# Hyena mixer of a hybrid encoder: Pool's elementwise work moves to VectorE, and a DMA that adds makes the weights' low parts

## The chip, the cores and the metric

The kernel runs on one core of one Trainium2 chip. The metric is the device time of one execution in microseconds; the time before is the median of three runs, and a change of 0.2% (2.5 us) is about what can be told from no change.

The engines are named as in the profile: PE (TensorE, matrix products; PEld is its weight load), DVE (VectorE), ACT (ScalarE), POOL (GpSimd) and SP (SyncE, which here only issues DMAs). They run their own instruction lists in order and wait for each other through semaphores. 16 DMA engines move data between HBM and the on-chip memory.

## The reference

The input is 256 tokens of 1024 channels in float32. Four layers follow, each `x = x + mixer(rmsnorm(x))`, then `x = x + swiglu(rmsnorm(x))`. The mixers are A, B, C, A: A is a gated short convolution, B is neighbourhood attention, C is Hyena. What matters here is A's and C's short convolution, and C's long one:

```python
def short_conv_mixer(h, w_in, conv_w, w_out):
    b_gate, c_gate, u = jnp.split(h @ w_in, 3, axis=-1)
    return (b_gate * depthwise_conv3(c_gate * u, conv_w)) @ w_out
...
def hyena_mixer(h, w_in, short_w, short_b, ...):
    v, x1, x2 = jnp.split(depthwise_conv3(h @ w_in, short_w, short_b), 3, axis=-1)
    h_freq = hyena_filters(seq, ...)
    def long_conv(u, n):
        y = irfft(rfft(u, n=2 * seq) * h_freq[:, n], n=2 * seq)[:, :seq]
        return y + u * f_skip[n]
    z = x1 * long_conv(v, 0)
    z = x2 * long_conv(z, 1)
    return z @ w_out
```

## The kernel before, in words

**Weights in two parts.** Every weight is streamed once from HBM in pieces of [128, 1024] float32 (512 KB). `wload` (L95) makes of a piece `st` two operands of float32r, a format of fewer bits that PE takes at full rate: ACT writes `hi`, the piece rounded (L105), and DVE, or POOL for a share of the pieces, writes `lo = st - hi` (L109, through the helper `tt`, L74). A product is then three matmuls (`mm3`, L113): hi by x's high part (L116), hi by x's low part (L117), lo by x's high part (L118). A piece makes 24 matmuls. There are 5 buffers for `st` and 6 each for `hi` and `lo`; a buffer is written again when its last reader is done.

**The spectra of the filters** are computed beside the first two SwiGLUs and kept in HBM (`hf`).

**Mixer C** runs at about 626 to 781 us. Its work is a list of pieces: 24 of `c_w_in`, numbered 0 to 23 here, then 8 of `c_w_out`, 24 to 31. After each piece `line.tick()` runs the stages that are due (`Pipeline`, L236; slots in `HYENA_SLOTS`, L44). The first four pieces are multiplied side by side, as the residual's tiles come in; then follow the norm's statistics (`stats`, L158, in which POOL computes 1 / rms as `rtm`, L171) and `expand` (L173). Channels go by quarters q of 256. `short(i, q)` scales the product (`cp`, DVE) and convolves each half with `conv3` (L331). `spectrum(o, q)` multiplies by the transform's matrix (`uf`, PE), then by the filter's spectrum `H` (tiles `hq`): with `U`, `a`, `b` of [128, 1024], DVE does two sums U (L74), the products a and b, and U's first half from a; POOL does U's second half from b and the two halves of the folded result `a`. `back` transforms back (`yi`, PE, L734 and L738), and `gate` multiplies by the next signal. `conv3` is one ACT instruction for the middle tap, one DVE `scalar_tensor_tensor` for the first (L338), one ACT instruction into `cr` for the third (L341), and one POOL addition of `cr`. In mixer C from tick 9 on, POOL makes 0.6 of the low parts.

**Mixer A** uses `conv3` too, once for each of 8 channel tiles in each of two layers, and has nothing else on POOL but the norm.

A scheduler sets the order on every engine from the order of the code and its own estimates, so the order can differ from that of the source.

Of the kernel before, what the change touches and what calls it, by code (L numbers as in the profile page):

```python
# [13 lines left out]
ALU = mybir.AluOpType  # L14
# [15 lines left out]
# columns of the per-partition vector table  # L30
# [9 lines left out]
# Where the stages of the pipelined work lie, in slots of one weight piece each.  # L40
FILTER_SLOTS = (range(0, 19, 2), range(2, 17, 2))  # within the first and the second SwiGLU
ATT_LAGS = (3, 0, 4, 5, 8, 11)  # bias, normed, features, scores, turned, values_out
V_LAG = 3
HYENA_SLOTS = (4, 5, 8, 11, 13, 16, 19)  # into, (spectrum, back, gate) twice  # L44
NORM_LAG = 1
AHEAD = 6  # rows of an output projection that are taken as they come
# The share of the weights' low parts that the Pool engine makes, where DVE has much to do
POOL_FILTERS, POOL_HYENA, POOL_HYENA_FROM = 0.17, 0.6, 9
# [3 lines left out]
def encoder(ctx: ExitStack, tc: tile.TileContext, A: dict, out: bass.AP):  # L52
# [23 lines left out]
    def v2(a):  # L76
        """[P, 512] as two halves."""
        return a.rearrange("p (i t) -> p i t", i=2)

# [13 lines left out]
    share, count = [0], [0]  # L93

    def wload(src, n, tag="", cuts=((0, None, None),)):  # L95
        """A piece of a weight, [P, n], as two float32r parts. It may be loaded in
        cuts (from, to, what else to do after it)."""
        st = wst.tile([P, D], F32, tag="st", name=f"st{tag}")
        hi = wsp.tile([P, D], F32R, tag="hi", name=f"hi{tag}")
        lo = wsp.tile([P, D], F32R, tag="lo", name=f"lo{tag}")  # L100
        for c0, c1, then in cuts:
            c = slice(c0, c1 or n)
            for dst, s in src if isinstance(src, list) else [(slice(None), src)]:
                sy.dma_start(out=st[dst, c], in_=s[:, c])
            ac.copy(out=hi[:, c], in_=st[:, c])  # L105
            count[0] += 1
            pool = int(count[0] * share[0]) > int((count[0] - 1) * share[0])
            tt(lo[:, c], st[:, c], hi[:, c].bitcast(F32), ALU.subtract, gp if pool else ve)
            if then is not None:  # L109
                then()  # L110
        return hi, lo
# [8 lines left out]
    def split(hl, src):  # L120
        """hl[:, 0] + hl[:, 1] = src, both float32r; the parts lie along axis 1."""
        ac.copy(out=hl[:, 0], in_=src)
        tt(hl[:, 1], src, hl[:, 0].bitcast(F32), ALU.subtract)

    class Norm:
        """The pre-norm of the next sub-layer: x times the gain as the operand of
        its products, and 1 / rms by token for what comes out of them."""
# [30 lines left out]
        def stats(self):  # L158
            """1 / rms, the tokens on the partitions."""
            n = self.name  # L160
            for m in self.late:
                self.square(m)
            ps = self.ps = bank(f"psn{n}")
            ms = tp.tile([P, 2], F32, tag="ms", name=f"ms{n}", bufs=2)
            for i in range(2):
                pe.transpose(ps[:, i * P : (i + 1) * P], self.ss[:, i * P : (i + 1) * P], ident)
            ve.tensor_reduce(out=ms, in_=ps[:, :T].rearrange("p (i f) -> p i f", i=2), axis=AX.X, op=ALU.add)
            ve.tensor_scalar(out=ms, in0=ms, scalar1=1.0 / D, scalar2=EPS,
                             op0=ALU.mult, op1=ALU.add)
            rt = self.rt = tp.tile([P, 2], F32, tag="rt", name=f"rt{n}", bufs=2)  # L170
            gp.tensor_tensor(out=rt, in0=ms, in1=nhalf[:, :2], op=ALU.pow)  # L171

        def expand(self):  # L173
            """1 / rms along the tokens, on every partition."""
            n, ps, rt = self.name, self.ps, self.rt
            for i in range(2):
                pe.transpose(ps[:, T + i * P : T + (i + 1) * P], rt[:, i : i + 1].broadcast_to([P, P]), ident)
            self.R = tp.tile([P, T], F32, tag="R", name=f"R{n}", bufs=2)
            ac.copy(out=self.R, in_=ps[:, T:])
# [9 lines left out]
    def in_tile(ps, w, norm):  # L189
        """One 128-column tile of a product with the normed input."""  # L190
        for n, (k, xs) in enumerate(norm.xs.items()):
            mm3(ps, w, slice(k * P, (k + 1) * P), xs[:, 0], xs[:, 1], n == 0, n == KT - 1)

    def in_group(parts, norm):
        """Several column tiles side by side, for the first products after a norm:
        (accumulator, weight, whether it is the first of its bank)."""
# [5 lines left out]
    class OutProj:  # L202
        """x += mid @ w, the rows of w as they come."""
# [20 lines left out]
        def finish(self, mids, norm):  # L224
            for k in range(self.ahead, KT):
                self.load(k)
            for m in [*range(0, KT, 2), *range(1, KT, 2)]:  # neighbours share a bank
                for k in range(self.ahead, KT):
                    self.mul(m, k, mids[k])
                residual(m, self.acc[m // 2][:, (m % 2) * T : (m % 2 + 1) * T], norm)  # L230
# [5 lines left out]
    class Pipeline:  # L236
        """Work in stages, each some slots after the one before it."""
# [12 lines left out]
        def tick(self):  # L250
            """The stages that are due, the oldest work first."""
# [60 lines left out]
    def triple(w, m, norm, name, ready, each=lambda i: None):  # L312
        """Column tiles m, KT + m, 2 KT + m. The first three with a norm go side by side,
        unless it is ready."""
# [16 lines left out]
    def conv3(y, src, wcol, step, m, bcol=None):  # L331
        """Depthwise convolution of width 3 along the tokens."""
# [7 lines left out]
        r = t1("cr")  # L340
        ac.activation(r, src, AF.Copy, scale=w[2])  # L341
        tt(y[:, : T - 1], y[:, : T - 1], r[:, 1:], ALU.add, gp)

# [32 lines left out]
    def mixer_b(norm, nxt):  # L376
        with tc.tile_pool(name="attc", bufs=1) as cp, tc.tile_pool(name="attw", bufs=2) as wp:
# [21 lines left out]
            def values(i, ps):  # L399
                """v of two head pairs, and for each block of query columns its keys (row by  # L400
                column) on the partitions."""
# [15 lines left out]
            def normed(m):  # L417
                """q and k by token, normed: the root mean squares of the tokens and of the
                heads in one factor."""
# [15 lines left out]
            def features(m):  # L435
                """q, the heads as blocks of a diagonal, and k, by feature."""
# [56 lines left out]
            def rows(k, ps, w, first):  # L493
                """Rows k of the weight: 256 columns of the product, by token."""
# [45 lines left out]
    hf = {(o, q): dram.tile([P, 2, 512], F32, name=f"hf{o}{q}") for o in range(2) for q in range(4)}  # L540

    def filters(cp, wp):
        """The filters' spectra at the 256 odd multiples of pi / 512: the lower 128
        from the sum, the upper 128 (mirrored, conjugate) from the difference of what
        the even and the odd times give."""
# [40 lines left out]
        # rows 0..63 the high part, rows 64..127 the low part  # L586
# [7 lines left out]
        for o in range(2):  # L594
            for q in range(4):
                if q % 2 == 0:
                    # two quarters of both directions
# [46 lines left out]
                # the skip is one more tap at time 0  # L644
# [8 lines left out]
    def mixer_c(norm, nxt):  # L653
        with tc.tile_pool(name="hyc", bufs=1) as cp, tc.tile_pool(name="hyw", bufs=2) as wp:
# [9 lines left out]
            def short(i, q, ps):  # L664
                """The short convolution of signal i of the quarter."""
# [7 lines left out]
            def by_time(q, i):  # L673
                """The signal with the times on the partitions, the even ones and the odd ones."""
# [24 lines left out]
            def spectrum(o, q):  # L699
                """The spectrum, times the filter's, folded for the even and the odd times."""  # L700
# [19 lines left out]
                tt(U[:, :, 1], b[:, :, 0], b[:, :, 1], ALU.add, gp)  # L720
                tt(a[:, 0], U[:, 0], U[:, 1], ALU.add, gp)
                tt(a[:, 1], U[:, 0], U[:, 1], ALU.subtract, gp)
                d["eo"] = a

            def back(o, q):
# [4 lines left out]
                for k in range(2):  # L730
                    for i in range(2):
# [3 lines left out]
                        else:  # L735
                            # by channel
# [14 lines left out]
            for i in range(3):  # L751
                for q in range(4):
                    ps = bank(f"ci{q}_{i}")
                    for j in range(2):
                        m = 2 * q + j
                        share[0] = POOL_HYENA if line.now >= POOL_HYENA_FROM else 0
# [18 lines left out]
            while line.todo:  # L775
                line.tick()
            op.finish(mids, nxt)

# [41 lines left out]
def _consts():  # L820
# [14 lines left out]
    # the frequencies below pi / 2; the others are their mirror images  # L835
# [4 lines left out]
    # [even times, odd times] x [frequency, (cosine, sine) by time]  # L840
# [20 lines left out]
    # what the sums of squares of q and of k are scaled by (the scores' 1 / 8 with q), and their guards  # L861
# [10 lines left out]
def _cols(w):  # L872
    """[L, K, N] -> [L, N / 128, 128 (K in), K / 128 * 128]: a column tile at a time."""
# [5 lines left out]
def _diagonals(rpb):  # L879
    """[heads, dr, dc] -> [head pair, (head parity, q row reversed, q column reversed),  # L880
    (block of q columns, k row, k column)]: shifted copies, so that each query has its row of biases."""
    w = np.lib.stride_tricks.sliding_window_view(rpb, 48, axis=2)[:, :, :16]
    w = np.stack([w[:, r + 4 : r + 4 + ROWS] for r in range(ROWS)])  # r, head, k row, i, j
# [4 lines left out]
def _layout(i):  # L888
# [5 lines left out]
    # by two head pairs: q and k of the one, of the other, then v of both  # L894
# [36 lines left out]
```

## Time and profile before

| | |
|---|---|
| runs | 1257.56, 1257.49, 1256.13 us; median 1257.49 |
| profiled execution | span 1256.2 us; its own time is not given apart from the span |
| PE | 1219.3 us busy, 97% of the span |
| DVE, ACT, POOL | 913.4 us (73%), 634.6 us (51%), 269.8 us (21%) |
| HBM read | 220.99 MB, 181 GB/s over the span |
| mean granted TensorE clock | 0.990 of full speed |

Busy time is an average over stages with different limits. The granted clock is the share of full speed that PE was given. Matmuls are pipelined: one of 256 columns shows about 280 ns from start to end, though the next starts about 120 ns after it. A row of waits names the instruction that waited, then the one that it waited for.

### The profile page before, as it was taken

The numbers are of one execution on the slowest core, as the hardware profiler recorded it, in microseconds if no ns is written. First come the engines' busy times: TensorE is split into PE (matmuls) and PEld (weight loads), VectorE is DVE, ScalarE is ACT, GpSimd is POOL, SyncE is SP. The second block draws the span as 40 slices with busy tenths as digits, with TensorE's granted clock in tenths as the row PEclk, the third lists the DMA queues.
The fourth block names the chain that finished last, engine by engine and source line by source line (L and its number), as shares of the span: only waits on it lengthen the run. The fifth ranks groups of instructions, "written<-read, shape, count | busy, mean of one in ns | idle before, by whom it ended". The sixth has DMA issues, their size and how long they took to land.

```text
span 1256.2 us, 24460 instructions
## 1 busy us (share of the span) xinstructions
PE 1219.3 (97%) x10034; PEld 1211.2 (96%) x10034; DVE 913.4 (73%) x1156; ACT 634.6 (51%) x931; POOL 269.8 (21%) x228
## 2 busy tenths in 40 slices
PE   7999999999999999999988979999999999999998
PEld 7999999999998999999988879999999999999998
DVE  7766877887776688878869997766655676766642
ACT  6545554555667554545544345444444455444431
POOL 0111122333454023213347773000000000000000
PEclk9999999999999999999998989999999999999999
DMA  9556556666666365666754324655566565655571
GB/s 307 184 175 229 185 173 193 201 191 222 209 178 194 118 218 186 192 187 191 232 179 135 121 98 155 199 184 185 173 185 197 176 188 163 199 185 185 170 203 46
DMA packets 68505, 228.90 MB, mean 182 GB/s; under 512 B 9831, under 2 KB 11241, under 8 KB 68265
## 3 DMA queue, kind: packets, MB, share of 16 engines
q1 hardware_dynamic: 61408, 211.68, 53.8%
q0 software_dynamic: 4656, 9.73, 2.6%
q10 hardware_dynamic: 2328, 5.93, 1.4%
q8 instruction: 78, 1.28, 0.4%
q14 instruction: 35, 0.28, 0.1%
HBM read 220.99 MB, written 6.29 MB: 181 GB/s over the span
## 4 chain that ended last, share of the span: by engine, by line
PE 84%; DVE 8%; issue 2%; ACT 2%; DMA 2%; POOL 2%; SPq 0%; ACTq 0%; DVEq 0%; POOLq 0%
PE pu L116 7%; PE pg L116 7%; PE pg L118 7%; PE pu L117 7%; PE pg L117 7%; PE pu L118 7%; PE po L116 7%; PE po L118 7%; PE po L117 7%; DVE a L74 1%; PE ai1a L117 1%; PE ai1a L116 1%; PE ai1a L118 1%; PE accao L116 1%; PE accao L117 1%
## 5 line engine op out<-in xcount | busy, mean ns | idle before, releaser
L105 ACT CAST hiw<-stw 128x1024 fp32r<-128x1024 f32 (+1 forms) x276 | 280.5, 1024 | 314.3 <-PE pg L117 85.3
L74 DVE TENSOR_TENSOR low<-stw,hiw 128x1024 fp32r<-128x1024 f32 (+1 forms) x254 | 306.2, 1212 | 155.1 <-ACT hiw L105 153.8
L116 PE MATMUL pu<-xsf,hiw 128*128 128x256 f32 x704 | 199.9, 284 | 0.0
L116 PE MATMUL pg<-xsf,hiw 128*128 128x256 f32 x704 | 199.3, 283 | 0.0
L118 PE MATMUL pg<-xsf,low 128*128 128x256 f32 x704 | 199.2, 283 | 0.0
L117 PE MATMUL pu<-xsf,hiw 128*128 128x256 f32 x704 | 199.2, 283 | 0.0
L117 PE MATMUL pg<-xsf,hiw 128*128 128x256 f32 x704 | 199.2, 283 | 0.0
L118 PE MATMUL pu<-xsf,low 128*128 128x256 f32 x704 | 199.2, 283 | 0.0
L116 PE MATMUL po<-hid,hiw 128*128 128x256 f32 x704 | 197.5, 281 | 0.0
L117 PE MATMUL po<-hid,hiw 128*128 128x256 f32 x704 | 197.5, 281 | 0.0
L118 PE MATMUL po<-hid,low 128*128 128x256 f32 x704 | 197.5, 281 | 0.0
L116 PEld LDWEIGHTS pg<-xsf,hiw 128*128 128x128 f32 x704 | 134.6, 191 | 0.3 <-issue 0.3
L116 PEld LDWEIGHTS pu<-xsf,hiw 128*128 128x128 f32 x704 | 134.5, 191 | 0.3 <-ACT hiw L105 0.3
L118 PEld LDWEIGHTS pg<-xsf,low 128*128 128x128 f32 x704 | 134.6, 191 | 0.0
L117 PEld LDWEIGHTS pg<-xsf,hiw 128*128 128x128 f32 x704 | 134.6, 191 | 0.0
L117 PEld LDWEIGHTS pu<-xsf,hiw 128*128 128x128 f32 x704 | 134.6, 191 | 0.0
L118 PEld LDWEIGHTS pu<-xsf,low 128*128 128x128 f32 x704 | 134.5, 191 | 0.0
L116 PEld LDWEIGHTS po<-hid,hiw 128*128 128x128 f32 x704 | 132.4, 188 | 0.0
L117 PEld LDWEIGHTS po<-hid,hiw 128*128 128x128 f32 x704 | 132.4, 188 | 0.0
L118 PEld LDWEIGHTS po<-hid,low 128*128 128x128 f32 x704 | 132.4, 188 | 0.0
L74 POOL TENSOR_TENSOR low<-stw,hiw 128x1024 fp32r<-128x1024 f32 (+1 forms) x22 | 53.6, 2434 | 158.8 <-ACT hiw L105 150.8
L105 ACT CAST hiai<-stai 128x1024 fp32r<-128x1024 f32 (+1 forms) x49 | 49.0, 1014 | 49.0 <-issue 13.3
(246 smaller groups left out, 2922.3 us busy)
## 6 DMA issues: line engine op xcount, KB each, us to landing
stw<-in_f_w SPq DMA_DIRECT2D x208, 512.0 KB, 3.6
stw<-in_f_w SPq DMA_DIRECT2D x64, 448.0 KB, 3.4
stai<-in_a_w_in SPq DMA_DIRECT2D x45, 512.0 KB, 3.7
stbi<-in_b_w_qkv SPq DMA_DIRECT2D x24, 512.0 KB, 4.3
stci<-in_c_w_in SPq DMA_DIRECT2D x24, 512.0 KB, 4.0
stao<-in_a_w_out SPq DMA_DIRECT2D x16, 512.0 KB, 4.3
hf<-ht POOLq DMA_DIRECT2D x16, 256.0 KB, 2.7
stbo<-in_b_w_out SPq DMA_DIRECT2D x8, 512.0 KB, 4.0
```

What stands on the lines that cost most here:

```text
L74: (eng or ve).tensor_tensor(out=out_, in0=a, in1=b, op=op)
L105: ac.copy(out=hi[:, c], in_=st[:, c])
L116: pe.matmul(ps, hi[:, ws], xh, start=first, stop=False, **kw)
L117: pe.matmul(ps, hi[:, ws], xl, start=False, stop=False, **kw)
L118: pe.matmul(ps, lo[:, ws], xh, start=False, stop=last, **kw)
```

## The change

Three things change (comments and docstrings, which the change also drops, are left out of the diff).

1. In `conv3`, in mixers A and C, the third tap becomes a second DVE `scalar_tensor_tensor`; ACT's `cr` and POOL's addition go.
2. In `spectrum`, POOL's three additions go to DVE.
3. In mixer C, for the pieces from tick 5 on (5 to 23 of `c_w_in` and 24 to 29 of `c_w_out`, 25 in all), neither DVE nor POOL makes the low part: ACT writes minus the rounded piece into `lo`, and a DMA issued by POOL reads the piece from HBM a second time and adds it to `lo` in place. The last two pieces are DVE's again.

```diff
-POOL_FILTERS, POOL_HYENA, POOL_HYENA_FROM = 0.17, 0.6, 9
+POOL_FILTERS = 0.17
+LOW_DMA_FROM = 5
...
             ac.copy(out=hi[:, c], in_=st[:, c])
+            if low_dma[0]:
+                ac.activation(lo[:, c], st[:, c], AF.Copy, scale=-1.0)
+                gp.dma_start(out=lo[:, c], in_=src[:, c], accum_op=ALU.add)
+                continue
             count[0] += 1
             pool = int(count[0] * share[0]) > int((count[0] - 1) * share[0])
             tt(lo[:, c], st[:, c], hi[:, c].bitcast(F32), ALU.subtract, gp if pool else ve)
...
         ve.scalar_tensor_tensor(out=y[:, 1:], in0=src[:, : T - 1], scalar=w[0], in1=y[:, 1:],
                                 op0=ALU.mult, op1=ALU.add)
-        r = t1("cr")
-        ac.activation(r, src, AF.Copy, scale=w[2])
-        tt(y[:, : T - 1], y[:, : T - 1], r[:, 1:], ALU.add, gp)
+        ve.scalar_tensor_tensor(out=y[:, : T - 1], in0=src[:, 1:], scalar=w[2], in1=y[:, : T - 1],
+                                op0=ALU.mult, op1=ALU.add)
...
-                tt(U[:, :, 1], b[:, :, 0], b[:, :, 1], ALU.add, gp)
-                tt(a[:, 0], U[:, 0], U[:, 1], ALU.add, gp)
-                tt(a[:, 1], U[:, 0], U[:, 1], ALU.subtract, gp)
+                tt(U[:, :, 1], b[:, :, 0], b[:, :, 1], ALU.add)
+                tt(a[:, 0], U[:, 0], U[:, 1], ALU.add)
+                tt(a[:, 1], U[:, 0], U[:, 1], ALU.subtract)
...
-                        share[0] = POOL_HYENA if line.now >= POOL_HYENA_FROM else 0
+                        low_dma[0] = line.now >= LOW_DMA_FROM
                         w = wload(A["c_w_in"][0][i * KT + m], D, f"ci{i}_{m}")
...
             while line.todo:
                 line.tick()
+            low_dma[0] = False
             op.finish(mids, nxt)
```

How the instructions move, at three places of mixer C. Lines of the changed kernel are 5 or 6 higher (its `tt` is L75, its `conv3` L343 to L346); in the names, the number after `loci_` is the channel tile.

POOL at the start of mixer C, before:

```order
L649 DMA hf_92<-ht_7770 128x512
L649 DMA hf_92<-ht_7773 128x512
L171 TENSOR_TENSOR rtm_8106<-msm_8101,nhalf 128x2
L74 TENSOR_TENSOR loci_1_8408<-stci_1_8406,hici_1_8407 128x1024
L74 TENSOR_TENSOR cx_0_8145<-cx_0_8145,cr 128x255 x2
```

and now, where L109 and L110 are the new ACT instruction and the new DMA:

```order
L654 DMA hf_92<-ht_7754 128x512
L654 DMA hf_92<-ht_7757 128x512
L110 DMA loci_5_8155<-in_c_w_in 128x1024
L110 DMA loci_6_8225<-in_c_w_in 128x1024
L177 TENSOR_TENSOR rtm_8090<-msm_8085,nhalf 128x2
L110 DMA loci_7_8264<-in_c_w_in 128x1024
```

Two of the adding DMAs stand ahead of the norm's `rtm`, and from there on POOL's list holds nothing but adding DMAs until the next norm.

ACT in the middle of mixer C, before:

```order
L105 CAST hici_6_8728<-stci_6_8727 128x1024
L741 COPY y_8392<-yi_8391 128x512
L122 CAST u_8398<-ut_0_8399 128x512
L704 DMA hq_8577<-hf_88 128x1024
L105 CAST hici_7_8765<-stci_7_8764 128x1024
L337 ACTIVATE cx_1_8438<-cp_1_8436,vec 128x256
L341 ACTIVATE cr<-cp_1_8436,vec 128x256
L337 ACTIVATE cx_1_8438<-cp_1_8436,vec 128x256
L341 ACTIVATE cr<-cp_1_8436,vec 128x256
L714 COPY e_8468<-uf_8451 128x512
```

and now:

```order
L106 CAST hici_6_8693<-stci_6_8692 128x1024
L746 COPY y_8364<-yi_8363 128x512
L128 CAST u_8370<-ut_0_8371 128x512
L109 ACTIVATE loci_6_8694<-stci_6_8692 128x1024
L106 CAST hici_7_8731<-stci_7_8730 128x1024
L709 DMA hq_8544<-hf_88 128x1024
L109 ACTIVATE loci_7_8732<-stci_7_8730 128x1024
L343 ACTIVATE cx_1_8411<-cp_1_8409,vec 128x256 x2
L719 COPY e_8437<-uf_8420 128x512
```

Each `hici` is followed, at once or after some instructions of the signals' chain, by the `loci` of the same piece, and the two `cr` are gone.

DVE for one spectrum and one short convolution, before:

```order
L74 TENSOR_TENSOR U_8593<-e_8596,uf_8586 128x512 x2
L74 TENSOR_TENSOR a_8594<-U_8593,hq_8577 128x1024
L74 TENSOR_TENSOR b_8595<-U_8593,hq_8577 128x1024
L74 TENSOR_TENSOR loci_2_8973<-stci_2_8971,hici_2_8972 128x1024
L74 TENSOR_TENSOR U_8593<-a_8594 128x2x256
L74 TENSOR_TENSOR cp_1_8674<-ci_1_8606,Rm_8141 128x512
L338 SCALAR_TENSOR_TENSOR cx_1_8676<-cp_1_8674,vec,cx_1_8676 128x255 x2
```

and now:

```order
L75 TENSOR_TENSOR U_8560<-e_8563,uf_8553 128x512 x2
L75 TENSOR_TENSOR a_8561<-U_8560,hq_8544 128x1024
L75 TENSOR_TENSOR b_8562<-U_8560,hq_8544 128x1024
L75 TENSOR_TENSOR cp_1_8643<-ci_1_8573,Rm_8125 128x512
L75 TENSOR_TENSOR U_8560<-a_8561 128x2x256
L75 TENSOR_TENSOR U_8560<-b_8562 128x2x256
L75 TENSOR_TENSOR a_8561<-U_8560 128x512 x2
L344 SCALAR_TENSOR_TENSOR cx_1_8645<-cp_1_8643,vec,cx_1_8645 128x255 x2
L346 SCALAR_TENSOR_TENSOR cx_1_8645<-cp_1_8643,vec,cx_1_8645 128x255 x2
```

The low part is gone from between the products and U's halves; U's second half, the two halves of `a` and the second `scalar_tensor_tensor` of each half have come.

## Rows read from the trace of the kernel before

**Rows 1.** The page: the span, and PE's busy time, share and instructions.
```profile
span 1256.2 us, 24460 instructions
...
PE 1219.3 (97%) x10034; PEld 1211.2 (96%) x10034; DVE 913.4 (73%) x1156; ACT 634.6 (51%) x931; POOL 269.8 (21%) x228
```

**Rows 2.** Windows: busy us (instructions) per engine, granted clock, DMA share and rate.
```profile
core 0: us, PE busy (x) PEld busy (x) DVE busy (x) ACT busy (x) POOL busy (x), PEclk, DMA share, GB/s
...
638.10:780.80 142.70, 123.95 (x902) 120.17 (x901) 127.89 (x125) 70.37 (x116) 97.37 (x63) 0.92 0.42 133
...
643.50:764.00 120.50, 103.14 (x728) 99.56 (x727) 110.82 (x102) 56.99 (x96) 91.98 (x61) 0.90 0.39 124
...
905.00:1005.00 100.00, 100.00 (x842) 100.00 (x841) 60.99 (x83) 47.26 (x64) 2.61 (x4) 1.00 0.61 185
...
610.00:620.00 10.00, 10.00 (x87) 10.00 (x87) 6.92 (x9) 4.40 (x6) 2.37 (x4) 1.00 0.90 306
```

**Rows 3.** Waits of PE, 638.1 to 780.8 us: total, times, longest.
```profile
PE yi L738 <- POOL a L74: 9.2, 5, 3.4
...
PE uf L117 <- DVE u L74: 5.5, 2, 3.0
...
PE psnm L177 <- POOL rtm L171: 1.4, 1, 1.4
```

**Rows 4.** Lines of DVE, 638.1 to 780.8 us: busy us, mean ns, idle before.
```profile
L338 DVE SCALAR_TENSOR_TENSOR cx<-cp,vec,cx 128x255 f32<-128x255 f32 x24 | 29.4, 1255 | 2.6 <-ACT cx L337 2.6
...
L74 DVE TENSOR_TENSOR a<-U,hq 128x1024 f32<-128x1024 f32 x8 | 19.8, 2477 | 0.2
...
L74 DVE TENSOR_TENSOR b<-U,hq 128x1024 f32<-128x1024 f32 x8 | 12.3, 1542 | 0.0
...
L74 DVE TENSOR_TENSOR loci<-stci,hici 128x1024 fp32r<-128x1024 f32 x9 | 11.9, 1324 | 9.0 <-ACT hici L105 9.0
...
L74 DVE TENSOR_TENSOR U<-a 128x512 f32<-128x512 f32 x8 | 8.4, 1051 | 0.2
```

**Rows 5.** DVE by tile, whole run: min/median/max ns, first and last start.
```profile
L74 DVE TENSOR_TENSOR a<-U,hq x8: 1225/2760/3452, 654.1 to 744.5; 128x1024 f32<-128x1024 f32 x8
...
L74 DVE TENSOR_TENSOR U<-a x8: 691/692/1784, 660.7 to 748.3; 128x512 f32<-128x512 f32 x8
...
L338 DVE SCALAR_TENSOR_TENSOR y<-u,vec,y x16: 476/478/480, 33.3 to 1042.5; 128x255 f32<-128x255 f32 x16
```

**Rows 6.** ACT and POOL by tile, whole run: min/median/max ns, first and last start.
```profile
L341 ACT ACTIVATE cr<-cp,vec x24: 492/493/497, 644.8 to 760.4; 128x256 f32<-128x256 f32 x24
...
L105 ACT CAST hici<-stci x24: 1032/1047/1057, 614.0 to 723.6; 128x1024 fp32r<-128x1024 f32 x24
...
L74 POOL TENSOR_TENSOR y<-y,cr x16: 637/640/645, 33.9 to 1043.1; 128x255 f32<-128x255 f32 x16
```

**Rows 7.** DMA: 638.1 to 764 us (two rows), 612 to 620 us, POOL's issue.
```profile
DMA packets 4258, 15.62 MB, mean 124 GB/s; under 512 B 464, under 2 KB 464, under 8 KB 4248
...
stw<-in_f_w SPq DMA_DIRECT2D x3, 512.0 KB, 3.3
...
dfth<-in_dfth POOLq DMA_DIRECT2D x1, 512.0 KB, 6.7
...
L656 POOL DMA_DIRECT2D dfth<-in_dfth x1: 564/564/564, 611.7 to 611.7; - x1
```

**Rows 8.** Timeline of POOL and of DVE about 621 us: start, duration, instruction.
```profile
621.00 1.15 POOL L649 DMA_DIRECT2D hf<-ht  x2 [1.02 <-DVE ht L74]
...
621.23 1.22 DVE L74 TENSOR_TENSOR loci<-stci,hici 128x1024 fp32r<-128x1024 f32 x1
```

**Rows 9.** Timeline of ACT and POOL at 637 us; PE by tile, mixer C's last products.
```profile
637.08 3.90 ACT L105 CAST hici<-stci 128x1024 fp32r<-128x1024 f32 x4 [8.67 <-PE ci L117]
...
641.01 1.61 POOL L171 TENSOR_TENSOR rtm<-msm,nhalf 128x2 f32<-128x2 f32 x1 [18.86 <-DVE msm L168]
...
L118 PE MATMUL accco<-midC,loco x64: 279/281/285, 758.2 to 780.6; 128*128 128x256 f32 x64
```

More of the change, by code (lines that the diff above doesn't have):

```diff
@@ L90, in encoder @@
     sy.dma_start(out=vec, in_=A["vec"])
-    share, count = [0], [0]
+    share, count, low_dma = [0], [0], [False]
     def wload(src, n, tag="", cuts=((0, None, None),)):
```

## The prediction

> **What bounds the kernel now.** I read the page first: PE is busy 1219.3 us of a span of 1256.2 us [rows 1], so only a stage in which PE waits or runs at a lower clock can give anything. The windows show the stage. From 905 to 1005 us PE is never idle and its granted clock is 1.00. From 638.1 to 780.8 us, mixer C from the norm on, it is busy 123.95 us of 142.7 at a mean granted clock of 0.92, a mixture of its two levels, 2.4 and 1.2 GHz [rows 2]. That is 18.75 us of idle time, and some 0.08 x 142.7 = 11.4 us that full clock would give back. PE's own work there is thus about 123.95 - 11.4 = 112.5 us.
>
> Next, who ends PE's waits: mostly POOL's halves of `a` (9.2 us) and DVE's `u` (5.5 us) [rows 3]. DVE is nearly full: 110.82 us of the 120.5 from 643.5 to 764 us [rows 2]. It is full because its instructions are long. The convolution's `scalar_tensor_tensor` takes 1255 ns, product a 2477 ns, b 1542 ns and U's half 1051 ns [rows 4], where the same instruction takes 478 ns in mixer A, and a and U's half 1225 and 691 ns at their shortest [rows 5]. POOL is busy 97.37 us of this stage and 2.61 us of the 100 from 905 us [rows 2]. So DVE is stretched while POOL works, and PE waits for the two of them.
>
> **The change, part by part.** All sums stand against the profiled span, 1256.2 us; the median of the runs is 1257.49, 1.3 us more. I subtract gains from the median.
>
> *Mixer A.* DVE gains 16 x 478 ns = 7.6 us over two layers, ACT loses 16 `cr` of the same form as the row shown, at 493 ns, and POOL loses 16 x 640 ns [rows 5, 6]. I cost it at nothing: the second mixer A lies around 1000 us, where PE is never idle while DVE is busy only 61 us in 100 [rows 2], and the chain from u to z loses one engine. Without that cover it would cost 7.6 us at most.
>
> *DVE in mixer C.* Without POOL's arithmetic the stretch goes: 24 x (1255 - 478) = 18.6 us, a 8 x (2477 - 1225) = 10.0, b 8 x (1542 - 1225) = 2.5 (a's form), U 8 x (1051 - 691) = 2.9, the low parts 9 x (1324 - 1220) = 0.9 [rows 4, 5, 8], together 34.9. These nine low parts themselves go: 9 x 1.22 = 11.0. Added are 24 `scalar_tensor_tensor` at 478 ns = 11.5 us and 24 half sums (8 for U, 16 for a) at 691 ns = 16.6 us. DVE goes from 127.9 to about 127.9 - 34.9 - 11.0 + 28.1 = 110 us.
>
> *ACT.* 25 more passes over a piece at 1.05 us, less 24 `cr` at 0.49 us [rows 6]: +14.5 us, from 70.4 to about 85 of 142.7 us. It stays off the path. What stands behind ACT's new instruction are the signals' casts, but it needs `st`, which is there already, and a `lo` buffer that PE frees with the same piece's `hi`, for which ACT waits before as well.
>
> *POOL.* 97 us of arithmetic become 25 issues at 0.56 us [rows 7]. `rtm` now stands behind two adds. The second needs piece 6's new pass. ACT reaches piece 6 at 637.1 us, as the row of four casts shows [rows 9], and is done with both passes at 639.2; the add is issued by 639.8. In the run before `rtm` began at 641.01 [rows 9], so nothing is lost.
>
> *The adds.* They load the DMA queues, and here lies the uncertainty. In mixer C from 638.1 to 764 us 15.62 MB move, 1.57 of them the next SwiGLU's three pieces [rows 7], which can come later: 14.05 MB are needed. 24 adds of 0.524 MB follow 639.8 us: 12.6 MB, times f, what an added byte costs against a loaded one. No row shows an adding DMA. The lower end is f = 1, the plain POOL load of 512 KB that landed in 6.7 us under load [rows 7]. The upper end I set at 3: as if reading the source, reading the old value and writing the sum each took as long as a plain transfer. I take the middle, f = 2. The Trainium skill (Collectives: The Full Stack, "The bandwidth ceiling: the fold count and why AG ≠ RS ≠ AR") says that a reducing DMA step needs two source reads a chunk, so half the rate. By it f is 2 and the sum is as below; no run here shows it.
>
> What the queues can do: at a share of 0.90 they moved 306 GB/s [rows 2], 340 GB/s when full. With f = 2 they need (14.05 + 25.2) / 0.34 = 115 us after 639.8. After the last add (piece 29) PE still has three pieces, 72 matmuls at 100 us / 842 = 0.119 us [rows 2], 8.6 us. PE ends at 639.8 + 115.4 + 8.6 = 763.8 us, where it now ends at 780.9 [rows 9]. This is later than PE's own 638.1 + 112.5 = 750.6, so the queues would set the pace, with DVE (110) and PE (112.5) close behind. A single add may take 10 us without harm: six `lo` buffers leave five pieces of work, at 112.5 us over 28 pieces some 20 us, between a buffer's release and its next use. What comes after mixer C keeps its length.
>
> **The sum:** -17.1 us; 1257.5 - 17.1 = 1240.4 us.
>
> **The rivals.**
>
> *Adds are cheap (f up to 1.5).* The queues are done by about 740 us and PE with DVE sets the pace. PE's work, the norm's wait of 1.4 us and half of the 14.7 us of waits for `a` and `u` [rows 3], as DVE is still nearly as full as PE, give 638.1 + 112.5 + 1.4 + 7.3 = 759.3: -21.6 us, 1235.9. For it: a POOL load of the same size looks ordinary.
>
> *Adds are dear, and it is slower.* The point is where the last add lands 8.6 us before 780.9: 132.5 us x 0.34 = 45.05 MB, less 14.05, over 12.6: f = 2.46. At f = 3 PE ends at 639.8 + 152.5 + 8.6 = 800.9: +20 us, 1277.5. At f = 2.8 it is +12.5 us. PE would then stand at the low parts while DVE idles. Against it only the shape speaks: long rows of 4 KB, as in a plain load. Within 0.2% of no change lies the narrow strip of f from 2.40 to 2.53.
>
> *Adds are held up by DVE.* POOL would be kept from preparing them while DVE works, and they would run only in DVE's gaps, 33 of 142.7 us, 23%. Even at f = 1, 24 adds of 1.54 us in 23% of the time take 161 us: PE ends at 809.1, +28.2 us, 1285.7. Against it: two POOL issues took 1.15 us together, about 0.56 each as usual, beside a DVE low of 1.22 us, also as usual [rows 8]. The Trainium skill (SBUF — State Buffer, "SBUF: two separate sides") has such a rule, that a DMA from GpSimd starves while VectorE runs one of its two-port modes. That row speaks against it here.
>
> *It does not relieve DVE.* If the stretch were not POOL's doing, DVE would need 127.9 - 9 x 1.32 + 24 x 1.255 + 24 x 1.051 = 171 us and be slower by some 30 us. Mixer A's equal 478 ns in all 16 cases makes this nearly impossible; it shares the last chance.
>
> **How the numbers follow.** Forecast (f about 1.5 to 2.4) 0.38, cheap 0.30, the strip of no change 0.06, dear 0.22, held up or not relieved 0.04. So faster 0.68, same 0.06, slower 0.26. The predicted time is the forecast's, 1240.4. The range reaches down to 1230, where PE would have hardly a wait (750.6 + 1.4 + 1.5 us, -27.4), with 0.05 left below; and up to 1268, f = 2.75, with half of the dear cases and the last ones, 0.14, above. As cases of both signs hold chances, the forecast's own range is 1236 to 1255 (f from 1.5, where PE and DVE set the pace as in the cheap case, to 2.4).
>
> **What would show it.** Right: the `scalar_tensor_tensor` of mixer C near 478 ns and product a near 1.23 us; DVE about 110 us in the stage; PE's last products of mixer C end near 764 us; the DMA share there goes from 0.42 to near 0.9; PE's waits are for the adds into `lo`. Cheap: the share stays below 0.75 and PE's waits are still for DVE. Dear: adds land later and later through the stage, and PE waits for them at piece after piece. Wrong altogether: DVE's instructions stay long, or mixer A grows.

## The result, and the profile after

The changed kernel takes 1228.26 us (median of 4 runs, 1226.87 to 1229.28); the kernel before, on the same chip, 1257.53. The ratio is 0.9764, 95% interval 0.975 to 0.9778: 29.3 us less, where 17.1 were forecast and 1230 was the range's low end. The profiled execution took 1226.87 us.

The page of the changed kernel, its span and busy times [rows 1]:

```profile
span 1225.1 us, 24409 instructions
...
PE 1206.4 (98%) x10034; PEld 1200.5 (98%) x10034; DVE 889.6 (73%) x1209; ACT 639.5 (52%) x916; POOL 186.2 (15%) x175
```

PE has 12.9 us less busy time for the same 10034 instructions, which goes with the 11.4 us that the prediction put down to the lower clock. Windows of the changed kernel, mixer C after the norm and the part of it in which the adds run:

```profile
core 0: us, PE busy (x) PEld busy (x) DVE busy (x) ACT busy (x) POOL busy (x), PEclk, DMA share, GB/s
638.10:752.00 113.90, 111.99 (x908) 110.37 (x907) 100.16 (x166) 83.47 (x118) 21.26 (x25) 1.00 1.00 278
640.00:735.00 95.00, 93.53 (x755) 92.12 (x754) 89.31 (x146) 71.91 (x100) 19.63 (x23) 1.00 1.05 285
```

In mixer C [rows 2] PE now idles 1.9 us of 113.9 at a granted clock of 1.00, the higher level, 2.4 GHz, where it idled 18.75 us of 142.7 at 0.92. POOL's 97 us are 21. The DMA engines went from a share of 0.42 to 1.00, and to 1.05 from 640 to 735 us (the shares of overlapping packets add up to a little over 1).

PE's waits from 625 to 760 us (total, times, longest) are all but gone [rows 3], and the last products of mixer C, by tile, end 31 us earlier [rows 9]:

```profile
PE ut L683 <- ACT cx L343: 0.8, 1, 0.8
PE uf L122 <- ACT u L128: 0.7, 1, 0.7
PE accco L124 <- DMA loco<-in_c_w_out: 0.4, 1, 0.4
```

```profile
L124 PE MATMUL accco<-midC,loco x64: 274/281/386, 726.4 to 749.5; 128*128 128x256 f32 x64
```

The lines of DVE and of POOL in 638 to 752 us (busy us, mean ns, idle before) show the short durations that the prediction counted on [rows 4]: 481 ns, 1223 and 684 in place of 1255, 2477 and 1051. An adding DMA occupies POOL for 0.87 us, where the issue shown of before took 0.56 [rows 7].

```profile
L344 DVE SCALAR_TENSOR_TENSOR cx<-cp,vec,cx 128x255 f32<-128x255 f32 x24 | 11.2, 481 | 1.6 <-ACT cx L343 1.6
L346 DVE SCALAR_TENSOR_TENSOR cx<-cp,vec,cx 128x255 f32<-128x255 f32 x24 | 11.0, 481 | 0.1
...
L75 DVE TENSOR_TENSOR a<-U,hq 128x1024 f32<-128x1024 f32 x8 | 9.8, 1223 | 0.2
L75 DVE TENSOR_TENSOR b<-U,hq 128x1024 f32<-128x1024 f32 x8 | 9.8, 1220 | 0.0
...
L75 DVE TENSOR_TENSOR U<-a 128x512 f32<-128x512 f32 x8 | 5.5, 684 | 0.0
```

```profile
L110 POOL DMA_DIRECT2D loci<-in_c_w_in x18 | 15.6, 868 | 57.0 <-ACT loci L109 54.0 <-ACT cx L343 2.9
L110 POOL DMA_DIRECT2D loco<-in_c_w_out x6 | 5.2, 864 | 22.9 <-ACT loco L109 18.4 <-issue 4.6
```

Last the DMA queues from 640 to 735 us: packets, MB, packet time as a share of the 16 engines' 95 us; then issues with KB and the median us to landing. q0 carries the adds, q1 SP's loads, q10 the filter spectra.

```profile
q0 software_dynamic: 3262, 11.92, 63.2%
q1 hardware_dynamic: 3264, 11.86, 33.3%
q10 hardware_dynamic: 864, 3.15, 8.2%
...
loci<-in_c_w_in POOLq DMA_DIRECT2D x17, 512.0 KB, 17.0
stci<-in_c_w_in SPq DMA_DIRECT2D x11, 512.0 KB, 15.2
```

An added MB takes 63.2% / 11.92 x 95 us = 5.04 us of all engines' time, a loaded one (33.3 + 8.2)% / (11.86 + 3.15) x 95 = 2.63 us. The ratio, the prediction's f, is 1.92. An add lands 17 us after its issue, and PE hardly waits for one.

### The profile page after: what moved, and what is told of

Read it like the earlier page. It is cut to its first block, busy times and chain, and to the rows that moved or that the text cites. A ratio compares the mean times of both kernels' runs of the same rounds, so it can differ in the third digit from the quotient of the medians.

```text
span 1225.1 us, 24409 instructions
## 1 busy us (share of the span) xinstructions
PE 1206.4 (98%) x10034; PEld 1200.5 (98%) x10034; DVE 889.6 (73%) x1209; ACT 639.5 (52%) x916; POOL 186.2 (15%) x175
## 4 chain that ended last, share of the span: by engine, by line
PE 91%; DVE 2%; DMA 2%; POOL 2%; ACT 1%; issue 1%; SPq 0%; POOLq 0%; DVEq 0%; ACTq 0%
PE pu L122 7%; PE pg L122 7%; PE pg L124 7%; PE pu L123 7%; PE pg L123 7%; PE pu L124 7%; PE po L124 7%; PE po L123 7%; PE po L122 7%; PE ci L123 2%; PE ci L122 2%; PE ci L124 2%; PE ai1a L123 1%; PE ai1a L122 1%; PE ai1a L124 1%; PE ai0a L123 1%
## 5 line engine op out<-in xcount | busy, mean ns | idle before, releaser
L75 DVE TENSOR_TENSOR low<-stw,hiw 128x1024 fp32r<-128x1024 f32 (+1 forms) x254 | 305.2, 1208 | 156.8 <-ACT hiw L106 155.4
L75 POOL TENSOR_TENSOR low<-stw,hiw 128x1024 fp32r<-128x1024 f32 (+1 forms) x22 | 53.5, 2432 | 215.3 <-ACT hiw L106 207.3
```

Source lines behind the costliest of these rows:

```text
L75: (eng or ve).tensor_tensor(out=out_, in0=a, in1=b, op=op)
```

## The experiments

**Which part gives the time.** Five variants have one half of the change or a piece of it. Ratios are to the kernel before, in runs beside it.

| low parts of mixer C | third tap | spectrum's sums | us | ratio (interval) |
|---|---|---|---|---|
| DVE and POOL (before) | POOL | POOL | 1257.5 | |
| DVE and POOL | DVE | DVE | 1257.3 | 0.9998 (0.9988 to 1.0007) |
| DVE alone | DVE | DVE | 1246.0 | 0.9912 (0.9892 to 0.9931) |
| adds | POOL | POOL | 1233.7 | 0.9811 (0.9796 to 0.9825) |
| adds | DVE | POOL | 1234.4 | 0.9819 (0.9802 to 0.9835) |
| adds | POOL | DVE | 1231.4 | 0.9786 (0.9772 to 0.9801) |
| adds (the change) | DVE | DVE | 1228.3 | 0.9764 (0.975 to 0.9778) |

*No adds, all low parts on DVE.* The changed kernel with one line edited:

```diff
-                        low_dma[0] = line.now >= LOW_DMA_FROM
+                        low_dma[0] = False
```

> Convolution and spectra on DVE as in the change, but every low part of mixer C on DVE, no adding DMA and no Pool. Theory A (the adds are needed because DVE would be the longest engine): DVE gets 25 low parts at 1.22 us, 30 us more, on the 100 us that it is busy from 638 to 752 us now, so about 130 us against PE's 112; the stage ends some 18 to 25 us later than in the change, 1245 to 1253 us, product a stays at 1.22 us. Theory B (Pool's reads were all the harm, and DVE has room for the low parts): within 4 us of the change, 1226 to 1232 us.

Measured 1246.0 us, in theory A's range. POOL does next to nothing, every DVE instruction is short, and still DVE is the bound: 109 of 114 us busy (a window of this kernel, columns as above).

```profile
638.00:752.00 114.00, 101.65 (x765) 97.74 (x764) 108.95 (x165) 52.00 (x77) 1.61 (x1) 0.96 0.37 124
```

*No adds, low parts by POOL and DVE as before.* The kernel before with the tap and the sums on DVE:

```diff
-        r = t1("cr")
-        ac.activation(r, src, AF.Copy, scale=w[2])
-        tt(y[:, : T - 1], y[:, : T - 1], r[:, 1:], ALU.add, gp)
+        ve.scalar_tensor_tensor(out=y[:, : T - 1], in0=src[:, 1:], scalar=w[2], in1=y[:, : T - 1],
+                                op0=ALU.mult, op1=ALU.add)
...
-                tt(U[:, :, 1], b[:, :, 0], b[:, :, 1], ALU.add, gp)
-                tt(a[:, 0], U[:, 0], U[:, 1], ALU.add, gp)
-                tt(a[:, 1], U[:, 0], U[:, 1], ALU.subtract, gp)
+                tt(U[:, :, 1], b[:, :, 0], b[:, :, 1], ALU.add)
+                tt(a[:, 0], U[:, 0], U[:, 1], ALU.add)
+                tt(a[:, 1], U[:, 0], U[:, 1], ALU.subtract)
```

> Convolution and spectra on DVE, but the low parts as before: 0.6 of them on Pool from tick 9 on, the rest on DVE, no adding DMA. Theory A (Pool's reads stretch DVE): 14 Pool low parts of 2.4 us hold DVE up by about 1.2 to 2.4 us each, 17 to 34 us, on top of 112 us of DVE work: DVE 130 to 145 us, 1245 to 1260 us. Theory B (Pool's low parts are harmless, only its sums on the chain were slow): 1230 to 1236 us.

Measured 1257.3 us, no change, as theory A has it. DVE's lines in 638 to 752 us, then POOL's: while POOL makes low parts, DVE is still stretched.

```profile
L74 DVE TENSOR_TENSOR loci<-stci,hici 128x1024 fp32r<-128x1024 f32 x9 | 12.8, 1420 | 8.8 <-ACT hici L105 8.8
...
L74 DVE TENSOR_TENSOR b<-U,hq 128x1024 f32<-128x1024 f32 x8 | 11.9, 1492 | 0.0
...
L74 DVE TENSOR_TENSOR U<-a 128x512 f32<-128x512 f32 x8 | 10.4, 1305 | 0.0
```

```profile
L74 POOL TENSOR_TENSOR loci<-stci,hici 128x1024 fp32r<-128x1024 f32 x9 | 25.7, 2861 | 48.0 <-ACT hici L105 48.0
```

*Adds alone.* The mirror image: the changed kernel with the last diff undone.

> The adding DMAs as in the change, but the third tap and the spectra's three sums stay on Pool (and ACT's cr stays). Theory A (any Pool arithmetic beside DVE stretches DVE): the convolution's instruction stays above 800 ns and product a above 1.6 us, PE still waits for Pool's a; about half of the gain, 1238 to 1250 us. Theory B (the low parts on Pool and DVE were the harm, the spectra's sums are small): 1226 to 1232 us, the convolution's instruction near 500 ns.

Measured 1233.7 us, between the two ranges: neither theory had its size right. The adds alone bring 24 of the 29 us, more than A had allowed; the rest is worth 5 us, more than B had. In the lines of DVE one instruction is still twice as long, the convolution's, while product `a`, which A put above 1.6 us, is short. PE waits a little for POOL's halves of `a` and for the tap:

```profile
L344 DVE SCALAR_TENSOR_TENSOR cx<-cp,vec,cx 128x255 f32<-128x255 f32 x24 | 24.4, 1041 | 5.3 <-ACT cx L343 5.2
...
L75 DVE TENSOR_TENSOR a<-U,hq 128x1024 f32<-128x1024 f32 x8 | 9.8, 1221 | 0.2
```

```profile
PE yi L744 <- POOL a L75: 2.1, 3, 1.6
PE ut L684 <- POOL cx L75: 1.2, 2, 0.6
```

*Tap and sums apart.* The last kernel with only the sums, or only the tap, left on POOL:

> The changed kernel with the spectra's three sums back on POOL; third tap on DVE, low parts by adds. The change with both on POOL lost 5.4 us (1233.7 against 1228.3). Theory S, the loss is the spectrum's chain on POOL (b, U's half, the two halves of a: 1.4 to 1.7 us each instead of 0.68): 1231 to 1235 here. Theory C, it is the convolution (DVE's cx was at 1041 ns there, the only instruction still long): within 1.5 us of 1228.3, and the cx at about 480 ns.

> The mirror of the last one: sums on DVE, third tap on POOL with its cr on ACT, low parts by adds. Theory S: within 1.5 us of 1228.3. Theory C: 1231 to 1235. Besides, if POOL's tensor_tensor is what makes the cx long, they are at 900 to 1050 ns here, and near 480 ns in the last one except where the sums of another signal run beside them.

Measured 1234.4 and 1231.4 us. The sums on POOL cost all that both cost together (S). The tap alone costs 3 us, over S's 1.5 and within C's range, but its interval overlaps the change's; so S holds for the sums, and the tap's part is not settled. The expected 900 to 1050 ns for the convolution's instruction beside the tap was wrong. The line of DVE with the sums on POOL (two instructions now), then with the tap on POOL:

```profile
L344 DVE SCALAR_TENSOR_TENSOR cx<-cp,vec,cx 128x255 f32<-128x255 f32 x24 | 20.0, 835 | 5.1 <-ACT cx L343 5.0
L346 DVE SCALAR_TENSOR_TENSOR cx<-cp,vec,cx 128x255 f32<-128x255 f32 x24 | 14.3, 606 | 0.2
```

```profile
L344 DVE SCALAR_TENSOR_TENSOR cx<-cp,vec,cx 128x255 f32<-128x255 f32 x24 | 13.2, 553 | 3.2 <-ACT cx L343 3.0
```

So it is mostly the sums, not the tap, that made it long. The timeline of the run with the sums on POOL bears this out: each `cx` that is long there (0.9 to 1.8 us) overlaps one of POOL's halves of `a`, and the others take 0.48 us; product `a` meets no arithmetic of POOL and takes 1.21 to 1.23 us.

*Mixer A alone.* The kernel before with the tap on DVE where there is no bias (mixer A):

```diff
+        if bcol is None:
+            ve.scalar_tensor_tensor(out=y[:, : T - 1], in0=src[:, 1:], scalar=w[2], in1=y[:, : T - 1],
+                                    op0=ALU.mult, op1=ALU.add)
+            return
```

> The kernel before with the third tap on DVE in mixer A alone; mixer C as before. The prediction costs this part at nothing: 1257 to 1258, within 2.5 us of before, and 16 cx-like instructions more on DVE at 478 ns in mixer A. The rival, that DVE's 7.6 us there are uncovered (or that one engine less in the chain gives something): over 2.5 us either way.

Measured 1257.06 us, 0.9995 (0.9985 to 1.0004), with 16 instructions of 484 ns added. Its cost of nothing stands.

**What sets the pace now: PE, or the queues?** *Copying instead of adding:*

```diff
-                gp.dma_start(out=lo[:, c], in_=src[:, c], accum_op=ALU.add)
+                gp.dma_start(out=lo[:, c], in_=src[:, c])
```

> The 25 adding DMAs become plain copies of the same piece into the low part, same queue, same place (so the low part is the piece itself and the result is not the reference's); ACT's pass stays. It measures what an added byte costs. If an add costs about twice a load (the change's trace: 11.92 MB of Pool's queue took 63.2% of the engines where 15.0 MB of the other two took 41.5%), the share of Pool's queue falls to 30 to 36% and landing from 17 us to below 8. Theory P (PE sets the pace in mixer C, the queue only just keeps up): time within 2 us of the change. Theory Q (the queue still sets part of the pace): 3 us or more faster.

Measured 1228.4 us, 0.9768 (0.9752 to 0.9784): the same as with adds, as theory P has it. Its window of mixer C, and its queues from 640 to 735 us:

```profile
638.00:752.00 114.00, 112.53 (x916) 111.15 (x916) 98.41 (x163) 83.70 (x116) 13.45 (x25) 1.00 0.81 277
```

```profile
q1 hardware_dynamic: 3335, 12.15, 38.7%
q0 software_dynamic: 3312, 12.06, 36.0%
q10 hardware_dynamic: 864, 3.15, 9.0%
...
loci<-in_c_w_in POOLq DMA_DIRECT2D x18, 512.0 KB, 5.5
```

The share falls to 0.81, transfers land in 5.5 us, and PE is no earlier: cheaper transfers would bring nothing, so PE sets the pace. Beside this copy on the same queue an add costs (63.2 / 11.92) / (36.0 / 12.06) = 1.78 times as much.

*More load on the queues.* The changed kernel with an extra load by SP into a scratch tile beside each add (shown for 512 KB):

```diff
                 gp.dma_start(out=lo[:, c], in_=src[:, c], accum_op=ALU.add)
+                ex = low_dma[1].tile([P, 1024], F32, tag="ex", name=f"ex{tag}", bufs=4)
+                sy.dma_start(out=ex, in_=src[:, :1024])
```

> The changed kernel, with one more plain load of 512 KB by SP, into a scratch tile of four buffers that nothing reads, beside each of the 25 adds (13.1 MB more). Theory T1, the queues are at their capacity and end level with PE: 13.1 MB at 381 GB/s (what the loads and adds of the changed kernel's own trace work out to when the share is full) is 34 us of queue time that nothing covers, so 1253 to 1264 us, and PE waits for loads or adds into hi and lo. Theory T2, the share of 1.0 only says that something is always queued, with much room left: under 1234 us, PE still without waits in mixer C.

> As the one before, with extra loads of 256 KB (6.6 MB in all). Theory T1: 17 us of queue time, less what little slack there is, 1238 to 1247 us. Theory T2: within 3 us of the changed kernel's 1228. If T1 holds in the larger one and not here, the slack lies between 0 and 17 us of queue time and the two times give it.

> As the kernels with extra loads, with 128 KB beside each add (3.3 MB in all) and 16 scratch buffers, so that an extra load seldom waits for a buffer in SP's order. 3.3 MB at 381 GB/s are 8.6 us of queue time. Theory T1 with the queues 2 us ahead of PE (as worked out from the changed kernel's trace: 100 us of transfers against 110 of PE's work, less the last three pieces): 1233 to 1237. The rival, that the 19 us of the 256 KB case were mostly SP's order (an extra load that waits for its buffer with the next piece's load behind it), and that the queues have 5 us or more to spare: 1228 to 1232.

Measured 1261.2, 1247.3 and 1238.7 us: the first in T1's range, the others just above it. But these runs do not settle it. SP's timeline of the 128 KB case shows 14 extra loads in a row, and then the load that ACT waits for:

```profile
635.18 12.97 SPq L112 DMA_DIRECT2D exci<-in_c_w_in  x14
650.74 0.33 SPq L105 DMA_DIRECT2D stci<-in_c_w_in  x1
```

ACT's wait for it (total, times, longest) holds up the cast of `u` behind it, for which PE then waits 6.7 us in one piece, the largest of its 8 us of waits in the stage:

```profile
ACT hici L106 <- DMA stci<-in_c_w_in: 9.9, 1, 9.9
```

That is SP's order, and tells nothing of the queues' capacity. So four more kernels pace the extras: a small copy by ACT ties each to its low part, and POOL issues it behind the add. The first has the small copy alone.

```diff
                 ac.activation(lo[:, c], st[:, c], AF.Copy, scale=-1.0)
+                ex = low_dma[1].tile([P, 256], F32, tag="ex", name=f"ex{tag}", bufs=16)
+                ac.copy(out=ex[:, :2], in_=lo[:, :2].bitcast(F32))
                 gp.dma_start(out=lo[:, c], in_=src[:, c], accum_op=ALU.add)
+                gp.dma_start(out=ex, in_=src[:, :256])
```

> Control of the next three: the changed kernel with ACT copying two columns of each low part into a scratch tile, and no extra transfer. Within 2 us of the changed kernel's 1228 if those 25 small copies are hidden, as ACT has some 30 of 114 us free in mixer C.

> The extra plain load of 128 KB a piece, now issued by POOL right behind the add and made to wait for the same pass of ACT, so that the extras come one a piece and never in SP's order (in the earlier kernels 14 of them stood in a row on SP at 635 to 648 us, ahead of loads that ACT needed). 3.3 MB at 2.8 us a MB (plain copies by POOL in the kernel without the adding took 36.0% of 95 us for 12.06 MB) are 9.3 us of queue time. Theory T1, queues level with PE: 6 to 11 us over the control. Theory T2, room of 9 us or more: within 2 us of the control. Theory T3, it is the number of transfers in flight from POOL (two a piece now, and POOL waits for an earlier one to land) and not the bytes that counts: a loss that is the same for 128, 256 and 512 KB.

> 256 KB a piece, paced in the same way: 6.55 MB, 18.6 us of queue time. T1: 15 to 21 us over the control. T2: at least 9 us less than the queue time, so under 10 us. T3: the same loss as with 128 KB, within 3 us.

> 512 KB a piece, paced in the same way (five scratch buffers, so ACT's small copy may wait for one): 13.1 MB, 37 us of queue time. T1: 33 to 42 us over the control. T2: under 28 us. T3: the same loss as with 128 KB, within 3 us.

Measured 1231.5 us for the control (3.2 more than the change, over the 2 expected; as the two intervals overlap, whether the small copy costs anything is open), then 1241.3, 1247.0 and 1262.4: 9.9, 15.5 and 30.9 us over the control. Their ratios to before, 0.9788, 0.9865, 0.9912 and 1.0033, have intervals of at most 0.0018 to either side. The loss grows with the bytes, so T3 falls, and there is no room of 9 us, so T2 falls as stated; T1 holds at 128 and 256 KB and is 2 us high at 512. From 256 to 512 KB the loss grows by 15.4 us for another 6.55 MB, 2.35 us a MB. PE's waits, of the 128 KB and then of the 512 KB case, are now for the adds, spread over many pieces:

```profile
PE accco L127 <- DMA loco<-in_c_w_out: 5.4, 4, 1.5
PE ci L127 <- DMA loci<-in_c_w_in: 2.4, 6, 0.6
```

```profile
PE ci L127 <- DMA loci<-in_c_w_in: 14.4, 14, 3.1
PE accco L127 <- DMA loco<-in_c_w_out: 8.3, 6, 2.9
```

Both limits thus lie level: without the adding PE is no faster, and with an extra quarter of an add's bytes beside each add PE waits.

*The sixth buffer.* The changed kernel and the kernel before with `bufs=5` in place of 6 in the pool of `hi` and `lo`:

> The changed kernel with five buffers of hi and of lo in place of six. Theory A, the adds' 16.8 us from issue to landing need the slack of six buffers (four pieces of PE's work behind a release are about 16 us, five are 20): 5 to 15 us more, 1233 to 1243, with PE waiting for adds into lo. Theory B, the landing time is only queueing and shrinks when fewer pieces are in flight: within 3 us of 1228.

> The kernel before with five buffers of hi and of lo, as the control of the last one. If five buffers cost something whatever makes the low parts, this is slower than 1257 by as much as the changed kernel is by its own loss; under theory A of the last one it is within 4 us of 1257, since here a low part is made in 1.3 to 2.7 us once its piece has landed.

Measured 1235.4 us, 0.9821 (0.9807 to 0.9836), against the change's 0.9764: 7 us more, theory A; PE waits for adds.

```profile
PE ci L124 <- DMA loci<-in_c_w_in: 6.6, 2, 5.7
PE accco L124 <- DMA loco<-in_c_w_out: 1.6, 2, 0.9
```

The kernel before loses nothing with five: 1255.1 us, 0.998 (0.997 to 0.999). The sixth buffer became necessary with the change.

## Why the prediction was wrong

The direction, the relief of DVE and f were right. What sets the end of the stage was not, and with it the size: the gain is 12 us larger than forecast and the time 1.7 us below the range. In the forecast the queues set the pace and PE waited for adds; measured, PE set it and waited 0.4 us for an add.

**Mixer A** at nothing: shown right. **DVE**: the stretch goes as costed. By the busy times of the lines, the terms of the sum took 18.7 us off, where 17.8 were forecast. Even so 110 us were forecast for the stage and 100.2 measured. Of the 10 us between them, 5 net are instructions that the sum left as they were and that were stretched too, above all the low parts of `c_w_out` and `midC`; their lines before, then now:

```profile
L74 DVE TENSOR_TENSOR loco<-stco,hico 128x1024 fp32r<-128x1024 f32 x3 | 5.2, 1723 | 0.0
L74 DVE TENSOR_TENSOR midC<-z,midC 128x512 fp32r<-128x512 f32 x4 | 4.9, 1224 | 0.0
```

```profile
L75 DVE TENSOR_TENSOR midC<-z,midC 128x512 fp32r<-128x512 f32 x4 | 2.7, 685 | 0.0
L75 DVE TENSOR_TENSOR loco<-stco,hico 128x1024 fp32r<-128x1024 f32 x2 | 2.4, 1224 | 0.1
```

Another 4 us are overlap: the lines add up to 134.0 us for 127.9 us busy before, and to 110.1 for 100.2 now. That 110.1 is also the forecast's number is chance. **ACT**: 85 forecast, 83.5 measured. **POOL**: 25 issues at 0.56 us forecast, 0.87 measured, with nothing behind them that PE waits for: psnm's wait of 1.4 us for `rtm` [rows 3] is gone from the rows above. **PE's own work** from 638.1 us to the end of mixer C: 112.5 forecast, 109.8 measured up to 749.8, with 890 matmuls in place of 902, as mixer C began 1.6 us earlier.

**The step that failed** is in "What the queues can do: at a share of 0.90 they moved 306 GB/s, 340 GB/s when full", and with it "the queues would set the pace". f = 2 was about right, 1.92 against loads and 1.78 against copies. But the rate priced a loaded MB at 2.94 us and an added one at 5.88, where 2.63 and 5.04 were measured. With these the queues need 14.05 x 2.63 + 12.58 x 5.04 = 100 us in place of 115.4, and PE ends at 639.8 + 100.4 + 8.6 = 748.8 in place of 763.8. PE's own end was put at 750.6; the last products began at 749.5. At the share of 1.05 at which the engines ran, the queues' sum would give 744. So the queues' end falls to about PE's own, and PE's decides. The trace has the end of the transfers itself, in POOL's issue of the last add and its time to landing:

```profile
730.45 0.86 POOL L110 DMA_DIRECT2D loco<-in_c_w_out  x1 [5.00 <-ACT loco L109]
...
loco<-in_c_w_out POOLq DMA_DIRECT2D x1, 512.0 KB, 10.7
```

It landed at 741.2, 101.4 us after 639.8 where the sum had 115.4, and the 8.6 us of PE's work behind it lead to 749.8. As its issue waited for ACT, this bounds the time that the queues needed from above only. From 763.8 to PE's own end of 750.6 are 13 of the 14 us by which the measured end is earlier. The paced loads price a MB without the shares, at 2.35 us between 256 and 512 KB, further still from 2.94. Of the 31 us by which the stage ends earlier in the two profiles, 1.6 are a start of mixer C at 624.8 in place of 626.4, less than its scatter over the kernels here (624.8 to 628.7).

Could the trace of before have told? Its DMA share and rate from 560 to 625 us, in 40 slices of 1.6 us:

```profile
DMA  8073360888797005999957286857308698999269
GB/s 247 28 181 141 49 234 5 203 226 275 210 363 277 30 0 88 375 223 375 312 160 251 35 267 153 201 232 204 129 15 270 212 310 239 383 381 292 86 242 290
```

Of the ten slices at a share of 0.9 or more (a 9), five moved 363 to 383 GB/s and the other five 223 to 312; the ten have a mean of 330. So 340 was a fair mean of full stretches in that trace; but its best slices moved more. At 380 GB/s the same sum reads 639.8 + 103.3 + 8.6 = 751.7, next to PE's own end. The prediction gave f two ends and the rate only one.

The **cheap rival** had the right picture of the end, PE setting the pace, but kept 8.7 us of waits; 1.9 were left. Its reason, DVE nearly as full as PE, failed with the 110: DVE had 100.2 us to do. The range's low end allowed for 2.9 us of waits and so was cut too close. The **dear rival** had f at 2.46 or more. The rule of the Trainium skill that stood beside the middle (Collectives: The Full Stack, "The bandwidth ceiling: the fold count and why AG ≠ RS ≠ AR"), half the rate for a reducing step that reads two sources, is near the 1.92 and 1.78 of this kernel. **Held up by DVE** did not occur: an issue takes 0.87 us while DVE is busy 89 of 95 us. By the Trainium skill (SBUF — State Buffer, "SBUF: two separate sides") a DMA issued from GpSimd starves while VectorE runs one of its two-port modes. This trace shows no starving, and no run here shows in which mode DVE ran. **Not relieving DVE** did not occur either; the run with POOL's low parts and everything else on DVE shows the stretch coming back with POOL's work.

The buffers: "a single add may take 10 us without harm", with 20 us of slack. The median add took 17 us and PE hardly waited; with one piece of slack less it did. That estimate was good, and nearer to its limit than the text says.

## What to carry to other kernels

Handing a subtraction to the DMA engines pays when it takes work off two engines that slow each other and the queues have idle time, but price the transfer in microseconds of all engines' time per MB, with both ends of the rate that full stretches show, and set it against the bound that comes next. Here PE and queues came out level, so further transfers in this stage, even 128 KB a piece, cost time at once. Long landing times are no loss by themselves: count the buffers between the producer and its user, and test with one less.

## What the runs showed of the hardware that was not expected

An adding DMA from HBM into SBUF took 1.78 times the engine time of a copy of the same size on the same queue, and POOL 0.87 us to issue, where the copy took 0.53. The engine time of a loaded MB isn't one number: 2.63 us for loads beside adds at a share of 1.05, against (38.7 + 9.0)% / 15.30 x 95 = 2.96 in the kernel with plain copies at a share of 0.84; the cause is open.

POOL's sums on 128x512 tiles made DVE's `scalar_tensor_tensor` take 835 ns in place of 481 while the product `a` kept its 1.22 us, as no sum ran beside it. Which of the two engines was held up went by which instruction began first, in all eight pairs of DVE's and POOL's halves of U in that run. Two of them, start and duration:

```profile
654.22 1.29 POOL L75 TENSOR_TENSOR U<-b 128x512 f32<-128x512 f32 x1
654.66 1.41 DVE L75 TENSOR_TENSOR U<-a 128x512 f32<-128x512 f32 x1
...
684.24 0.69 DVE L75 TENSOR_TENSOR U<-a 128x512 f32<-128x512 f32 x1
684.29 1.80 POOL L75 TENSOR_TENSOR U<-b 128x512 f32<-128x512 f32 x1 [1.52 <-DVE b L75]
```

In three pairs DVE's half began behind POOL's and took 1.39 to 1.41 us, POOL's 1.27 to 1.29. In the other five it began 0.05 us ahead and took 0.69, and POOL's took 1.78 to 1.80.
